# Token mixers cut into steps paced by dense tiles, block changes made token tile by token tile, and the operator set-up spread over two blocks

## The chip, the cores and the metric

One Trainium2 chip, one NeuronCore. The metric is device time of one execution in microseconds (us). The kernel before was run three times: 2354.3, 2359.55 and 2361.64 us, median 2359.55 us. One more execution was profiled and took 2362.64 us, 3.1 us more than that median; every duration read from the trace belongs to it.

## The reference, cut to what matters

One pre-norm layer over 2048 tokens of width 1024, in float32: a token mixer with four head groups of width 256, then a squared-ReLU MLP of width 4096.

```python
h = rmsnorm(x, norm_mix)
proj = h @ w_in                                  # 1024 x 2560
y_a = short_conv_mixer(cv_h, cv_b, cv_c, conv_w)         # A: gated convolution over 3 tokens
y_b = s5_mixer(s5_u, ...)                                # B: complex diagonal state space, scan, GELU, GLU
y_c = swa_sink_attention(a_q, a_k, a_v, ...)             # C: attention over 3 chunks of 64 tokens, with sinks
y_d = hgrn2_mixer(hg_q, hg_f, hg_i, hg_g, ...)           # D: gated linear recurrence, 4 heads of 64
y = rmsnorm(stack([y_a, y_b, y_c, y_d]), group_norm)
x = x + y @ w_out
h = rmsnorm(x, norm_ffn)
x = x + square(relu(h @ w_ff1)) @ w_ff2
```

B and D carry a state along the tokens, C reads the two chunks before its own, A the two tokens before.

## The kernel before, in words

**Dense work.** Every dense product is made of matmuls of 128x128 by 128x512. Each float32 operand is split into a high and a low part of a reduced type, and `mm3` (L485) adds three products: high by high (L486), high by low (L487), low by high (L488). A *dense tile* is one bank of 512 accumulated columns: 8 blocks of the contraction, so 24 matmuls. The 2048 tokens go in four blocks of 512. Per block and in `w_in`: `attn_in` (L668) 4 tiles, `hgrn_in` (L800) 4, `hgrn_in2` (L821) 4, `conv_group` (L516) 6, `s5_in` (L570) 2, so 20 tiles; then `outp` (L941) 8 tiles per block with `w_out`. That makes 112 tiles in the *mixer stage*. `attn_in`, `hgrn_in2` and `outp` go by token tile (`tm_tile`, L505: the 128 tokens are stationary, one tile reads one quarter of the activations); `hgrn_in`, `conv_group` and `s5_in` go by feature tile (`proj_fm`, L494: each reads all 512 tokens).

**Weights.** `load_split` (L98) loads a unit of 128x512, ACT writes the high part (L105), DVE the low part (L111). A tile needs two new units on average (224 units in all). Rings hold 6 raw units and 9 split ones. Matmul tiles have two PSUM banks (`mm`), transposes of activations one (`tr`), attention two (`mx`), the recurrence two (`hx`), the state space one (`sx`).

**Activations.** `hh` and `hl` (L140) hold one block's normalised, transposed, split activations, and there is one copy of them. `make_hT` (L464) fills them with 8 transposes per token tile through `tr`; `outp` fills the same two buffers with the mixers' outputs, 6 transposes per token tile through `hx` (L959, L963, L964), from rows that the mixers have stored to HBM.

**Mixers.** `attn` (L683) per token tile: norms, transposes, then per key head scores, softmax, transposes of the probabilities, product with the values. `hgrn` (L837) per half block: seven levels of doubling length, each of masked products (L877 to h=8, L880 above), their evacuation (DVE L886 or ACT L889), and three multiplies that prepare the next level (DVE L895, POOL L896, DVE L898), then state products. `s5_setup` (L211) computes the operators of the state space once, nearly all of it many short DVE instructions; `s5_step` (L580) takes two blocks at a time: eight channel groups, then eight gated-unit tiles, whose results go to HBM. `conv_finish` (L547) norms the convolution. `rstd_of` (L89) does every reciprocal root, on POOL.

**Order.** All of this is traced by Python generators, which `run` (L979) exhausts one after the other (L989 to L1041); a `yield` has no effect there. The order of tracing is the order of priority. A scheduler then gives each engine one fixed order: among the instructions whose inputs it reckons to be ready, the one with the highest priority goes first, and dense matmuls fill in where a mixer is reckoned to wait. `tc.high_priority()` lifts the weight splits and the evacuations; `first(HTP)` lifts `make_hT` above the rest of its block. Per block the list is: activations, dense tiles of attention and recurrence, `hgrn`, `attn`, then the convolution's and the state space's dense tiles, `s5_step` after blocks 1 and 3. `s5_setup` lies in block 0, `outp` after all blocks. SP issues every load and store from one queue.

After L1041 come the two MLP stages (`ff1` with L1189, the second product at L1319). The change does not touch them.

Of the kernel before, what the change touches and what calls it, by code (L numbers as in the profile page):

```python
# [21 lines left out]
P = 128  # L22
# [37 lines left out]
def emit(ctx, tc, a):  # L60
# [150 lines left out]
    def s5_setup():  # L211
        with tc.tile_pool(name="st", bufs=1) as st:
# [106 lines left out]
            dbl(cs, sn)  # L319

# [15 lines left out]
            for k in range(2, 9):  # L336
                h1, h2 = k // 2, k - k // 2
                cmul(pw[:, 0, :, k], pw[:, 1, :, k], pw[:, 0, :, h1], pw[:, 1, :, h1], pw[:, 0, :, h2], pw[:, 1, :, h2])
            rv = st.tile([P, 2, 8, 8], F32, name="rv")
            for k in range(8):  # L340
                V.tensor_copy(out=rv[:, :, :, k], in_=pw[:, :, :, 7 - k])

# [24 lines left out]
            tt(bb[:, 1], bb[:, 1], tb_, ALU.add)  # L367

# [11 lines left out]
            while n < P:  # L380
# [10 lines left out]
                n *= 2  # L391
            V.tensor_copy(out=rotN[:, 0, :], in_=ctab[:, :, P])
# [7 lines left out]
            def outer(xr, xi, pr, pi, neg):  # L400
# [3 lines left out]
                for q in range(2):  # L404
# [11 lines left out]
                    if neg:  # L416
                        stt(f3(o1), f3(o1), -1.0, f3(tmp), ALU.mult, ALU.subtract)
                    else:
                        tt(o1, o1, tmp, ALU.add)
                return o  # L420
# [3 lines left out]
            E = outer(cc[:, 0], cc[:, 1], pw[:, 0, :, 0:8], pw[:, 1, :, 0:8], True)  # L424
            tt(db, db, ident[0:16, 0:16].unsqueeze(1).to_broadcast([16, 16, 16]), ALU.mult)
            for q4 in range(4):
                H = st.tile([16, 4, 16, 8], F32, tag="H", name="H")
                for par in range(2):
                    ph = psum_sx()
                    rs = slice(par * 64, par * 64 + 64)  # L430
                    for gl in range(2):
                        gp = q4 * 2 + gl
                        for i_ in range(2):
# [3 lines left out]
                                  in_=ph[0:16, 0:256].rearrange("p (g n) -> p g n", g=2))  # L437
                tt(H[:, :, :, 0], H[:, :, :, 0], db[:, q4 * 4:(q4 + 1) * 4, :], ALU.add)
                for i_ in range(8):
                    Hs = st.tile([16, 4, 16, 8], F32, tag="Hs", name="Hs")  # L440
                    if i_ > 0:
# [3 lines left out]
                                 in_=Hs.rearrange("p (q g) h k -> p q (g h k)", g=2))  # L445

            E = outer(cc[:, 0], cc[:, 1], pw[:, 0, :, 1:9], pw[:, 1, :, 1:9], True)
# [6 lines left out]
            E = outer(bb[:, 0], bb[:, 1], rv[:, 0], rv[:, 1], False)  # L454
            for gp in range(8):
# [5 lines left out]
                SY.dma_start(out=two_d[:, gp, 2:4, :], in_=wsb)  # L461


    def make_hT(b):  # L464
        for i in range(4):
# [6 lines left out]
            V.scalar_tensor_tensor(out=xt, in0=xt, scalar=r, in1=g_mix, op0=ALU.mult, op1=ALU.mult)  # L472
            for k4 in range(2):
# [73 lines left out]
    def conv_finish(b):  # L547
# [4 lines left out]
        V.tensor_tensor(out=sq[0], in0=sq[0], in1=sq[1], op=ALU.add)  # L552
        pss = psum_tr()
        for i in range(4):
# [6 lines left out]
                        in1=r.unsqueeze(2).to_broadcast([P, 4, P]), op=ALU.mult)  # L561
        pb = psum_tr()
# [17 lines left out]
    def s5_step(s):  # L580
        newc = cm.tile([P, 8, 2], F32, tag="carry2", name="carry2")
        for gp in range(8):
# [27 lines left out]
            yield  # L610
# [9 lines left out]
            if s == 0:  # L620
# [4 lines left out]
                V.tensor_tensor(out=newc[:, gp, 1:2], in0=k1[:, 1:2], in1=k1[:, 2:3], op=ALU.add)  # L625
            py = psum_sx()
# [17 lines left out]
        for j in range(NCH):  # L644
            yt = s5p.tile([P, 2, P], F32, tag="yt", name="yt", bufs=2)
            SY.dma_start(out=yt, in_=g_d[s][:, j, :].rearrange("(c p) n -> p c n", p=P))
            yh = s5p.tile([P, 2, P], F32R, tag="yh", name="yh")
            yl = s5p.tile([P, 2, P], F32R, tag="yl", name="yl")
            S.activation(out=yh, in_=yt, func=AF.Copy)
            V.tensor_tensor(out=yl, in0=yt, in1=yh, op=ALU.subtract)  # L650
            pg = psum_sx()
            for ct in range(2):
                mm3(pg, yh[:, ct, :], yl[:, ct, :], wgh[:, ct, :], wgl[:, ct, :], ct == 0, ct == 1)
            th = s5p.tile([P, GW], F32, tag="ta", name="gth")
# [6 lines left out]
            yo = s5p.tile([P, GW], F32, tag="gyo", name="gyo")  # L661
# [21 lines left out]
    def attn(b):  # L683
# [4 lines left out]
        for i in range(4):  # L688
# [7 lines left out]
            sq = mix.tile([P, 384], F32, tag="qsq", name="qsq")  # L696
# [12 lines left out]
                            in1=r[:, 4:6].unsqueeze(2).to_broadcast([P, 2, 64]), op=ALU.mult)  # L709
            pt = psum_mx()  # L710
# [10 lines left out]
            for kv in range(2):  # L721
# [23 lines left out]
                pT = psum_mx()  # L745
# [617 lines left out]
```

## Time and profile before

| | |
|---|---|
| median of three runs | 2359.55 us |
| profiled execution, its own time | 2362.64 us |
| its span, first to last instruction | 2360.9 us |
| mixer stage, to the first MLP matmul | 0 to 1042 us |
| first MLP product | 1042 to 1728 us |
| second MLP product | 1728 to 2361 us |
| PE, DVE, ACT, POOL busy share of the span | 95%, 61%, 41%, 7% |

The span is the time that the trace covers; the 1.7 us between it and the execution's own time lie around it. "Busy" of PE counts a matmul from its start to its modelled end, and neighbours overlap, so a busy PE may still be one that waits for its pipeline. PEclk is the granted clock of TensorE as a share of 2.4 GHz; its other level is 1.2 GHz, so 0.75 over a stretch means that half of the stretch ran at the lower level.

### The profile page before, as it was taken

The numbers are of one execution on the slowest core, as the hardware profiler recorded it, in microseconds if no ns is written. First come the engines' busy times: TensorE is split into PE (matmuls) and PEld (weight loads), VectorE is DVE, ScalarE is ACT, GpSimd is POOL, SyncE is SP. The second block draws the span as 40 slices with busy tenths as digits, with TensorE's granted clock in tenths as the row PEclk, the third lists the DMA queues.
The fourth block names the chain that finished last, engine by engine and source line by source line (L and its number), as shares of the span: only waits on it lengthen the run. The fifth ranks groups of instructions, "written<-read, shape, count | busy, mean of one in ns | idle before, by whom it ended". The sixth has DMA issues, their size and how long they took to land.

```text
span 2360.9 us, 32548 instructions
## 1 busy us (share of the span) xinstructions
PE 2240.9 (95%) x11460; PEld 1751.5 (74%) x11460; DVE 1447.0 (61%) x3008; ACT 956.5 (41%) x1910; POOL 166.5 (7%) x208
## 2 busy tenths in 40 slices
PE   7899998999999998999999999999989999999999
PEld 6676776666777776777777767777768888888887
DVE  6688687887656775586656666766653344244342
ACT  4334333434434334465555564544543133133121
POOL 1130112023113000000000000000000000000000
PEclk9999997999999999999999999999999999999999
DMA  6313324441331566656566577888774554455542
GB/s 203 85 49 113 111 78 124 140 121 56 106 103 47 154 217 199 216 174 190 176 180 177 179 213 252 284 258 259 215 222 144 172 183 137 131 187 177 185 147 98
DMA packets 393347, 381.35 MB, mean 162 GB/s; under 512 B 35968, under 2 KB 310496, under 8 KB 393184
## 3 DMA queue, kind: packets, MB, share of 16 engines
q1 hardware_dynamic: 393184, 379.27, 51.8%
q8 instruction: 90, 1.47, 0.3%
q14 instruction: 73, 0.60, 0.1%
HBM read 261.77 MB, written 116.40 MB: 160 GB/s over the span
## 4 chain that ended last, share of the span: by engine, by line
PE 60%; DVE 10%; DMA 7%; ACT 4%; issue 3%; POOL 2%; SPq 0%; DVEq 0%; POOLq 0%; ACTq 0%
PE mm L1319 25%; PE mm L1189 10%; PE hx L1189 5%; PE mm L488 4%; PE mm L487 4%; PE mm L486 4%; DMA w2r<-in_w_ff_dram 2%; PE mx L1189 2%; DVE tp L1060 2%; ACT wh L1050 1%; DVE w2r L1060 1%; DMA fxs<-x1d 1%; DMA wr<-in_w_out_dram 1%; DVE wl L1051 1%; PE mx L778 1%
## 5 line engine op out<-in xcount | busy, mean ns | idle before, releaser
L1319 PE MATMUL mm<-wh,st 128*128 128x512 f32 x1792 | 561.9, 394 | 0.9 <-ACT X L1322 0.7
L1319 PEld LDWEIGHTS mm<-wh,st 128*128 128x128 f32 x1792 | 337.3, 188 | 79.8 <-ACT X L1322 1.2
L1319 PE MATMUL mm<-wl,st 128*128 128x512 f32 x896 | 353.5, 395 | 2.7 <-DVE wl L1051 2.7
L1189 PE MATMUL mm<-tb,wh 128*128 128x512 f32 x1024 | 330.0, 403 | 16.4 <-ACT tp L1202 6.7
L1290 ACT ACTIVATE st<-sr 128x1024 fp32r<-128x1024 f32 x112 | 114.6, 1054 | 404.2 <-PE mm L1319 359.2
L1189 PEld LDWEIGHTS mm<-tb,wh 128*128 128x128 f32 x1024 | 189.5, 191 | 77.2 <-ACT tp L1208 14.2
L487 PE MATMUL mm<-wl,hh 128*128 128x512 f32 x512 | 205.2, 401 | 4.8 <-DVE wl L111 4.8
L486 PE MATMUL mm<-wh,hh 128*128 128x512 f32 x512 | 206.9, 404 | 2.2 <-ACT hh L481 2.1
L1051 DVE TENSOR_TENSOR wl<-wr,wh 128x512 fp32r<-128x512 f32 x208 | 138.0, 687 | 113.6 <-ACT wh L1050 66.7
L488 PE MATMUL mm<-wh,hl 128*128 128x512 f32 x512 | 207.3, 405 | 0.0
L105 ACT ACTIVATE wh<-wr 128x512 fp32r<-128x512 f32 x224 | 138.6, 629 | 168.2 <-PE mm L487 111.7
L1189 PE MATMUL mm<-tb,wl 128*128 128x512 f32 x512 | 204.2, 399 | 0.0
L1319 PEld LDWEIGHTS mm<-wl,st 128*128 128x128 f32 x896 | 168.4, 188 | 43.1 <-DVE wl L1051 3.1
L1291 DVE TENSOR_TENSOR st<-sr,st 128x1024 fp32r<-128x1024 f32 x112 | 133.8, 1221 | 95.0 <-ACT st L1290 94.9
L111 DVE TENSOR_TENSOR wl<-wr,wh 128x512 fp32r<-128x512 f32 x224 | 152.4, 698 | 40.1 <-ACT wh L105 36.9
L1189 PE MATMUL hx<-tb,wh 128*128 128x512 f32 x512 | 162.4, 397 | 8.4 <-ACT wh L1050 8.4
L486 PE MATMUL mm<-hh,wh 128*128 128x512 f32 x384 | 157.1, 409 | 2.0 <-ACT QP L807 1.0
L488 PE MATMUL mm<-hh,wl 128*128 128x512 f32 x384 | 157.1, 409 | 0.0
L487 PE MATMUL mm<-hl,wh 128*128 128x512 f32 x384 | 156.3, 407 | 0.0
L1050 ACT ACTIVATE wh<-wr 128x512 fp32r<-128x512 f32 x208 | 125.7, 625 | 69.3 <-PE mm L1189 31.2
L1060 DVE TENSOR_TENSOR tq<-mm,tq 128x512 f32<-128x512 f32 x32 | 22.1, 691 | 173.6 <-PE mm L1319 173.4
L1195 ACT ACTIVATE tp<-tp 128x512 f32<-128x512 f32 x96 | 60.5, 630 | 157.1 <-DVE tp L1060 157.1
(372 smaller groups left out, 3638.3 us busy)
## 6 DMA issues: line engine op xcount, KB each, us to landing
as<-tp SPq DMA_DIRECT2D x224, 256.0 KB, 2.8
sr<-as SPq DMA_DIRECT2D x112, 512.0 KB, 4.3
wr<-in_w_ff_dram SPq DMA_DIRECT2D x176, 256.0 KB, 3.9
wr<-in_w_in_dram SPq DMA_DIRECT2D x160, 256.0 KB, 3.1
wr<-in_w_out_dram SPq DMA_DIRECT2D x64, 256.0 KB, 4.0
w2r<-in_w_ff_dram SPq DMA_DIRECT2D x32, 512.0 KB, 4.5
tt<-w2r SPq DMA_DIRECT2D x32, 512.0 KB, 3.3
wr<-tt SPq DMA_DIRECT2D x64, 256.0 KB, 4.2
```

Source lines behind the costliest of these rows:

```text
L105: S.activation(out=hi, in_=raw, func=AF.Copy)
L111: (G if le == "p" else V).tensor_tensor(out=lo, in0=raw, in1=hi, op=ALU.subtract)
L486: PE.matmul(ps, lhsT=lh, rhs=rh, start=first, stop=False)
L487: PE.matmul(ps, lhsT=lh, rhs=rl, start=False, stop=False)
L488: PE.matmul(ps, lhsT=ll, rhs=rh, start=False, stop=last)
L1050: S.activation(out=h, in_=raw, func=AF.Copy)
L1051: V.tensor_tensor(out=l, in0=raw, in1=h, op=ALU.subtract)
L1060: V.tensor_tensor(out=o, in0=x, in1=y, op=op)
L1189: PE.matmul(ps, lhsT=(wh, wl)[lw][:, ks], rhs=b[lb][:, k, :], start=first and k == 0 and q == 0, stop=k == 3 and q == 2, skip_group_check= ...
L1290: S.activation(out=s_[:, 0, ks], in_=r, func=AF.Copy)
L1291: V.tensor_tensor(out=s_[:, 1, ks], in0=r, in1=s_[:, 0, ks], op=ALU.subtract)
L1319: PE.matmul(ps, lhsT=st_[:, ls, k, :], rhs=tu[i, k][lt], start=k == 0 and p_ == 0, stop=k == NJ - 1 and p_ == 2)
```

## The change

The generators get more `yield`s, so that one step of a mixer is some PE work whose inputs were made in the step before, followed by the vector work for the next. A small driver replaces the list of `run` calls: after every dense tile, each mixer on a list of *tracks* advances by its own pace.

```diff
+    def track(gen, pace, key):
+        tracks.append([gen, pace, 0.0, key])
+    def advance():
+        for t_ in list(tracks):
+            t_[2] += t_[1]
+            while t_[2] >= 1.0:
+                t_[2] -= 1.0
+                if next(t_[0], "end") == "end":
...
+    def dense(g, side=None):
+        for _ in g:
+            if side is not None:
+                next(side, None)
+            advance()
...
+    for b in range(NB):
+        dense(attn_in(b))
+        drain("hg")
+        track(attn(b), 1.35, "at")
+        if b == 0:
+            track(s5_setup(), 1.5, "set")
+        if b == 2:
+            drain("set")
+            s5p = mixs.enter_context(tc.tile_pool(name="s5p", bufs=1, reuse_waits="tile"))
+            track(s5_step(0), 1.0, "s5")
+        if b == 3:
+            drain("s5")
+            dense(s5_in(b))
+            track(s5_step(1), 1.0, "s5")
+        dense(hgrn_in(b))
+        track(hgrn(b), 1.25, "hg")
+        dense(conv_group(b))
+        track(conv_finish(b), 0.5, "cv")
+        if b < 3:
+            dense(s5_in(b))
+        nxt = make_hT(b + 1) if b < 3 else out_in(0)
+        next(nxt)
+        dense(hgrn_in2(b), nxt)
+        run(nxt)
+        drain("at", "cv")
+    for b in range(3):
+        g = outp(b)
+        for _ in range(4):
+            next(g)
+            advance()
+        drain(*((), ("s5",), ("hg",))[b])
+        nxt = out_in(b + 1)
+        next(nxt)
+        dense(g, nxt)
+        run(nxt)
```

`drain` runs what is left of a track at once. The side generator makes the block change: after token tile i of `hgrn_in2` (or of the second half of `outp`) the next block's token tile i is transposed into the quarter of `hh` and `hl` that has just been read. Its load and norm are traced one tile ahead.

```diff
     def make_hT(b):
+        def norm(i):
...
+        nx = norm(0)
+        yield
+        for i in range(4):
+            xt = nx
+            if i < 3:
+                nx = norm(i + 1)
...
-    def outp(b):
+    def out_in(b):
...
+        nx = load(0)
+        yield
+        for i in range(4):
...
-                    pt = psum_hx()
+                pt = psum_tr()
```

In `hgrn` the two halves of a block now alternate level by level instead of following one another; a level is one step, and the state part waits until `hgrn_in2` has been traced.

```diff
-        for hf in range(2):
-            yield from hgrn_half(b, hf, QPs[hf], KQs[hf], Fgs[hf], ...)
...
+        for lv in range(7):
+            for hf in range(2):
...
+                bps[hf] = nbp
+                yield
+        while ("hv", b) not in st8:
+            yield
...
-            ke = mix.tile([P, GW], F32, tag="ke", name="ke", bufs=2)
+            ke = mix.tile([P, 2, GW], F32, tag="ke", name="ke")
```

`hacc` gets four buffers for two, the small products `bp` two for one. In `attn`, the load shift and the norm of token tile i+1 are traced in the last step of tile i before its probabilities are transposed, and there is a `yield` before the transposes of the probabilities and one after their evacuation. In `s5_step`, the gated unit's load and split (`glu_in`) are traced one tile ahead with two buffers, and the step boundary of a channel group lies after all its scan work. In `s5_setup` there are yields between its parts (some 45 steps). The priority lift of `outp`'s transposes goes; its evacuations keep theirs. The same products are computed; no arithmetic is added.

## Rows read from the trace of the kernel before

**Rows 1.** The page's head: span, busy time of engines, granted clock in 40 slices.
```profile
span 2360.9 us, 32548 instructions
...
PE 2240.9 (95%) x11460; PEld 1751.5 (74%) x11460; DVE 1447.0 (61%) x3008; ACT 956.5 (41%) x1910; POOL 166.5 (7%) x208
...
PEclk9999997999999999999999999999999999999999
```
**Rows 2.** Windows by stage: length, busy PE, PEld, DVE, ACT, POOL, clock, DMA.
```profile
0.00:13.00 13.00, 1.11 (x4) 0.71 (x4) 3.68 (x15) 5.42 (x9) 1.31 (x6) 1.00 0.71 246
13.00:200.00 187.00, 169.43 (x1105) 131.18 (x1105) 137.81 (x472) 71.81 (x190) 36.97 (x41) 0.95 0.36 99
200.00:390.00 190.00, 178.65 (x1156) 136.69 (x1154) 144.31 (x354) 69.06 (x176) 33.08 (x38) 0.92 0.36 102
390.00:610.00 220.00, 205.77 (x1408) 153.13 (x1407) 175.17 (x515) 93.40 (x266) 44.41 (x56) 0.99 0.38 110
610.00:785.00 175.00, 165.09 (x1161) 128.41 (x1160) 107.24 (x268) 70.95 (x194) 36.16 (x41) 1.00 0.29 87
785.00:1042.00 257.00, 241.23 (x1192) 186.28 (x1191) 174.66 (x385) 106.19 (x229) 10.18 (x18) 0.99 0.64 205
1042.00:1728.00 686.00, 654.80 (x2759) 509.92 (x2758) 448.93 (x698) 363.94 (x628) 4.39 (x8) 0.99 0.70 213
1728.00:2361.00 633.00, 624.82 (x2688) 505.17 (x2686) 255.24 (x307) 175.70 (x225) 0.00 (x0) 1.00 0.49 161
```
**Rows 3.** Windows inside the mixer stage: length, busy PE, PEld, DVE, ACT, POOL, clock, DMA.
```profile
100.00:175.00 75.00, 66.38 (x647) 50.77 (x644) 68.83 (x291) 28.87 (x94) 23.20 (x28) 1.00 0.15 45
350.00:400.00 50.00, 43.95 (x332) 33.73 (x332) 37.80 (x93) 15.36 (x44) 8.11 (x10) 0.73 0.41 113
...
525.00:600.00 75.00, 67.70 (x619) 50.70 (x618) 56.77 (x162) 33.53 (x111) 23.16 (x30) 1.00 0.21 59
...
650.00:675.00 25.00, 25.00 (x112) 20.71 (x111) 11.25 (x25) 8.73 (x20) 0.00 (x0) 1.00 0.46 139
...
925.00:940.00 15.00, 8.85 (x35) 6.69 (x34) 5.78 (x10) 3.81 (x8) 0.00 (x0) 0.78 0.83 286
```
**Rows 4.** Groups of instructions by line, whole run: busy us, mean ns, idle before.
```profile
L488 PE MATMUL mm<-wh,hl 128*128 128x512 f32 x512 | 207.3, 405 | 0.0
...
L488 PE MATMUL mm<-hh,wl 128*128 128x512 f32 x384 | 157.1, 409 | 0.0
...
L111 DVE TENSOR_TENSOR wl<-wr,wh 128x512 fp32r<-128x512 f32 x224 | 152.4, 698 | 40.1 <-ACT wh L105 36.9 <-ACT apr L741 1.5 <-PE mm L488 0.2
...
L886 DVE COPY_PREDICATED hacc<-masks,hx 128x512 f32<-128x512 uint8 x64 | 43.9, 725 | 8.8 <-PE hx L877 8.6
...
L964 DVE TENSOR_TENSOR hl<-hx,hh 128x384 fp32r<-128x384 f32 x32 | 17.2, 552 | 17.2 <-ACT hh L963 16.8
...
L963 ACT ACTIVATE hh<-hx 128x384 fp32r<-128x384 f32 x32 | 15.1, 487 | 31.8 <-PE mm L487 19.3 <-PE hx L959 11.5 <-PE mm L488 0.6
```
**Rows 5.** PE's waits from 13 to 785 us: total us, times, longest us.
```profile
PE hx L877 <- DVE QP L895: 7.3, 6, 2.3
PE mm L487 <- DVE wl L111: 4.8, 2, 2.6
...
PE tr L477 <- DVE hl L482: 2.6, 6, 0.8
```
**Rows 6.** Timeline of PE, 925 to 938 us: start, us, instruction, idle before it.
```profile
935.59 1.54 PE L959 MATMUL hx<-ident,ybt 128*128 128x128 f32 x6 [6.07 <-DMA ybt<-ybd]
```
**Rows 7.** Line L896, POOL's multiply of the recurrence: ns least, median, most.
```profile
L896 POOL TENSOR_TENSOR KQ<-KQ,bp x48: 614/688/955, 105.0 to 757.4; 128x256 f32<-128x256 f32 x48
```
**Rows 8.** SP's queue in the mixer stage: its longest wait in total.
```profile
SPq L102 <- DVE wl L111: 164.2, 115, 17.2
```

More of the change, by code (lines that the diff above doesn't have):

```diff
@@ L367, in s5_setup @@
             tt(bb[:, 1], bb[:, 1], tb_, ALU.add)
+            yield
             for _ in range(3):
@@ L687, in attn, with norm @@
             V.tensor_copy(out=kT[:, 0:P], in_=st8["ktail"])
-        for i in range(4):
+        def norm(i):
             ti = b * 4 + i
@@ L695, in attn @@
                 SY.dma_start(out=st8["vs"][64:128, :], in_=va[0:64, :])
-            sq = mix.tile([P, 384], F32, tag="qsq", name="qsq")
+            prev = (st8.get("va"), st8.get("vs"))
+            st8["va"], st8["vs"] = va, vs_next
+            sq = mix.tile([P, 384], F32, tag="qn", name="qsq")
             S.activation(out=sq, in_=qk, func=AF.Square)
@@ L744, in attn @@
                 V.reciprocal(out=rs_, in_=rs_)
-                pT = psum_mx()
-                pTs = mix.tile([P, 2, 2, P], F32, tag="pTs", name="pTs")
                 vvs = []
@@ L756, in attn @@
                     elif e == 0:
-                        parts = [(0, 128, st8["va"]), (128, 64, va)]
+                        parts = [(0, 128, va_prev), (128, 64, va)]
                     else:
-                        parts = [(0, 128, st8["vs"]), (128, 64, vs_next)]
+                        parts = [(0, 128, vs_prev), (128, 64, vs_next)]
                     vvs.append(parts)
-                    for pi, (o, kn, vv) in enumerate(parts):
+                if kv == 1 and i < 3:
+                    nx = norm(i + 1)
+                yield
+                pT = psum_mx()
+                pTs = mix.tile([P, 2, 2, P], F32, tag="pTs", name="pTs")
+                for e in range(2):
+                    for pi, (o, kn, vv) in enumerate(vvs[e]):
                         o2 = (pi * 2 + e) * P
@@ L983, in run @@
         return r
-    def hT(b):
-        with first(-4000 if b == 0 else HTP):
-            run(make_hT(b))
-    hT(0)
-    run(hgrn_in2(0))
-    run(hgrn_in(0))
-    run(attn_in(0))
-    run(hgrn(0))
-    run(attn(0))
-    s5_setup()
-    s5p = mixs.enter_context(tc.tile_pool(name="s5p", bufs=1, reuse_waits="tile"))
-    run(conv_group(0))
-    run(conv_finish(0))
-    run(s5_in(0))
-    hT(1)
-    run(attn_in(1))
-    run(hgrn_in(1))
-    run(hgrn_in2(1))
-    run(hgrn(1))
-    run(attn(1))
@@ L1006, in emit @@
-    run(conv_group(1))
-    run(conv_finish(1))
-    run(s5_in(1))
-    run(s5_step(0))
-    hT(2)
-    run(attn_in(2))
-    run(hgrn_in(2))
-    run(hgrn_in2(2))
-    run(hgrn(2))
-    run(attn(2))
-    run(conv_group(2))
-    run(conv_finish(2))
-    run(s5_in(2))
-    hT(3)
-    run(attn_in(3))
-    run(hgrn_in(3))
-    run(hgrn_in2(3))
-    run(hgrn(3))
-    run(attn(3))
-    run(conv_group(3))
-    run(conv_finish(3))
-    run(s5_in(3))
-    run(s5_step(1))
-    run(outp(0))
-    run(outp(1))
@@ L1031, in emit, with drain @@
-    run(outp(2))
+    tracks = []
+    def track(gen, pace, key):
[6 more added lines that the diff above has]
+                if next(t_[0], "end") == "end":
+                    tracks.remove(t_)
+                    break
+    def drain(*keys):
+        for t_ in list(tracks):
+            if t_[3] in keys:
+                run(t_[0])
+                tracks.remove(t_)
@@ new lines, in dense @@
+    def dense(g, side=None):
[3 more added lines that the diff above has]
+            advance()
+    with first(-4000):
+        run(make_hT(0))
+    s5p = None
+    for b in range(NB):
[23 more added lines that the diff above has]
+        drain("at", "cv")
```

274 lines of the change are left out of this document (152 added, 122 removed).

## The prediction

> **What bounds the kernel now.** I read the page's head first. PE is busy for 95% of the span, DVE for 61%, POOL for 7% [rows 1]. So only PE's idle time, its lower clock, and waits hidden inside its busy time can be won; no product is taken away.
>
> The windows by stage come next [rows 2]. The two MLP stages, 686 and 633 us, are not touched; there PE idles 686 - 654.8 = 31.2 us (4.5%) and 633 - 624.8 = 8.2 us (1.3%). In the mixer stage PE starts dense work at 13 us, and from there to 1042 us, 1029 us long, it is busy 169.4 + 178.7 + 205.8 + 165.1 + 241.2 = 960.2 us. It idles **68.8 us**, 6.7%. The stage's clock is also the only one with real dips: 0.95 over 187 us and 0.92 over 190 us lose 9.4 and 15.2 us of full-speed time, 0.01 of the 220 and 257 us another 4.8: **29.3 us** in all.
>
> Then where these lie [rows 3]. From 100 to 175 us DVE is busy 68.8 of 75 us (92%) and PE idles 8.6 us: block 0's recurrence, attention and the operator set-up are crowded there. From 650 to 675 us DVE works 45% and PE runs 112 matmuls in 25 us without a gap, 0.223 us each. The dense stage is 112 tiles of 24, 2688 matmuls: lines L488 count 512 + 384, and two sister lines as many each [rows 4], so 600 us at that rate, 5.36 us per tile. The other 360 busy us are small matmuls. What is wrong is the distribution: mixers come in lumps, with few dense tiles beside them, and pure dense stretches lie between.
>
> PE's waits name the chains [rows 5]: QP's multiply before a level's products, the split before a transpose's bank is free. Each is small. The largest single one is 6.07 us at 929 us, where the last output block's rows come back from HBM [rows 6].
>
> **The change, part by part.** All numbers are against the profiled execution's 2362.6 us, which lies 3.1 us above the median of 2359.55 that I predict from.
>
> *Pacing.* Dense tiles per block 20, 5.36 us each. `attn` has 22 steps at 1.35 per tile (16 tiles), `hgrn` 15 steps on 12 tiles at 1.25 and the rest on the next block's 4, `s5_setup` some 45 steps on 30 tiles, `s5_step` 25 on 20 to 26. So each step's inputs are about one tile older than its matmuls, against a DVE chain of two L886 (1.45 us) and a multiply, plus POOL's 0.69 us [rows 4, 7]. That covers the waits before small matmuls [rows 5], if DVE has no backlog. DVE's work stays at 739 us over the stage; on 970 us that is 76%, without the 92% lump. How much idle time stays, no row shows. The ends are the MLP stages' shares on 973 us: 44 us at 4.5%, where DVE is busy 65%, and 13 us at 1.3%, where it is busy 40% [rows 2]. With 76% it is nearer the first; I take (2 x 44 + 13)/3 = 34 us left, **35 us back**. Below: nothing back.
>
> *Clock.* The deepest dip, 0.73 from 350 to 400 us, came with PE busy 44 of 50 us but nearly all of that on small matmuls (332 matmuls where pure dense work shows 112 per 25 us); from 525 to 600 us dense tiles and small groups mix, and the clock is 1.00 [rows 3]. Paced steps are such a mix everywhere. Ends 0 and 29.3; nearest is the mixed row, so all but 5 us come back, **24 us**. The Trainium skill ("TensorE: Matmul & The Clock Gate", section "Why this matters for your kernels") puts drops down to idle gaps between bursts of matmuls. That agrees with the 6.07 us gap followed by 0.78 [rows 3, 6], not with the dip of a busy PE; by it only 0.22 x 15 = 3.3 us would come back and the sum would be 21 us worse.
>
> *Block change by token tile.* Before, the transposes of the next block wait for the last feature tile, which reads all 512 tokens; now each hides behind the next token tile's 24 matmuls. Its idle time is part of the 68.8. `out_in` moves from the two `hx` banks to the single `tr` bank: 16 token tiles, each with a second group that waits for ACT 0.49 + DVE 0.55 = 1.04 us [rows 4]: 0 to 16.6 us. `make_hT` lives with the same one bank and shows 2.6 us over its 16 tiles [rows 5]; I take **+3**. Queued behind such a transpose on PE are dense tile i+1 and the steps traced with it. Loads for the next tile join SP's queue one tile earlier; there they pass weight loads that mostly wait for a free raw buffer (164 us over 115 waits [rows 8]) and are early by 5.36 us, so nothing is added. The 6.07 us should mostly go: it needs the last gated unit's store, which the drain inside `outp(1)` puts just ahead of the load, so up to 1 or 2 us can remain; counted in the 34.
>
> *Drains.* A handful of steps are left at each: one of `hgrn`, one of `attn`, five gated-unit tiles in block 3. They run as chains, with dense tiles of `s5_in(3)` as cover; without it a 0.7 us DVE link each. **+1**.
>
> *Set-up spread, `norm` and `glu_in` a tile early.* The DVE count is the same; the short set-up instructions leave the stretch of 92%. Early norms put POOL's root ahead of recurrence multiplies on POOL, which is busy 162 of the 1029 us [rows 2]; cover is ample. The set-up's many small stores pass the weight loads in SP's queue over 30 tiles instead of 20; both are waited for a tile later. Merging two copies of `ke` into one, and alternating halves, save ACT time that nobody waits for. All nothing; if the cover goes, it is the price of the slower rival.
>
> *Inside busy time.* A small matmul whose predecessor feeds it is counted busy while its pipe fills. No row gives that share of the 360 us. Between 0 and one twentieth (18 us) could come back with fewer, longer groups; I take none and keep 18 for the range.
>
> **Sum:** -35 - 24 + 3 + 1 = -55 us: 2307.6 against 2362.6, so about **2304 us** against the median.
>
> **Rivals.**
>
> *Clock dips stay.* If small matmul groups pull the clock down wherever they are, only 3.3 of the 24 us return: 2304 + 21 = 2325. For it: 0.73 with PE busy. Against it: 1.00 in the mixed row. This is also where the skill's rule on idle gaps leads. Chance 0.12.
>
> *The order hardly changes.* The scheduler already mixes dense and mixer matmuls by readiness; tracing in other order may give the same interleaving, and DVE, not the order, makes the chains late. Then little beyond the 6 us gap returns: 2353. For it: 95% busy already. Against it: DVE at 92% and 45% in stretches of the same stage [rows 3]. Chance 0.12, half of it within 0.3% (7 us, about what a measurement can tell from no change).
>
> *Slower: mixer work on DVE in front of the weight split.* Now every dense tile has mixer instructions around it, in one DVE order with the split L111 (0.70 us, two per tile, nine buffers, of which a token tile group holds eight). If one L886 (0.725 us) is exposed per tile, 112 x 0.725 = 81 us come in against 55: 2386 us. It decides at 55/112 = 0.49 us per tile. Behind the late split stand the tile's 24 matmuls, its evacuation, and the raw buffer that SP's next weight load waits for. For it: 68.8 of 75 us where everything meets. Against it: until 785 us PE waits only 4.8 us in total for L111 [rows 5]. Chance 0.12. The Trainium skill ("SBUF — State Buffer", section "SBUF: two separate sides") has a further way to it: a GpSimd instruction and a DVE one with two SBUF inputs lock each other out of a shared port. L896 between 614 and 955 ns [rows 7] fits some of that, with POOL as the loser; no row shows DVE losing.
>
> *Larger gain.* Idle falls to 13 us (56 back), all 29 us of clock, no added cost: -85, 2275; with the 18 us inside busy time 2257. For it: 25 us without a gap at 650 us. Against it: nothing runs that smoothly with DVE above 70%. Chance 0.08.
>
> **How the numbers follow.** The forecast has 0.56 and lies between 2280 and 2335. Faster by over 0.3%: 0.56 + 0.12 + 0.06 + 0.08 = 0.82; same 0.06; slower 0.12. The range takes in the larger gain's end and the rivals up to no change: 2257 to 2360; left out are the slower rival and a little at either end.
>
> **What would show it.** The first L1189 matmul should come near 987 us instead of 1042, the MLP stages staying at 686 and 633. In windows of the mixer stage DVE should lie between 60 and 90% everywhere, PE's idle sum from 13 us near 34, the clock at 0.98 or more in each stage; waits of `hx` and `mx` matmuls for DVE should shrink and those of `tr` grow a little (L959's successor). It is wrong if PE's wait for L111 exceeds 50 us, if the clock stays at 0.95 or below in the first 400 us, or if an MLP stage moves by more than 5 us.

## The result, and the profile after

The change makes the kernel **faster by half a per cent**: median 2346.52 us of 16 executions (2338.22 to 2357.89) against 2359.86 us of 16 executions of the kernel before; ratio **0.9949**, 95% interval [0.9932, 0.9965]. That is 12 us by the ratio (13 between the medians) where 55 were forecast. The profiled execution has a span of 2341.6 us, 19.3 less than that of [rows 1]; its own time, 2343.7 us, lies 2.8 us under the median, and that of the profiled execution before 2.8 us above the median of its kernel, so the shares below add up to 19 and not to 12.

The page's head, to be read beside [rows 1]:

```profile
span 2341.6 us, 32446 instructions
...
PE 2227.5 (95%) x11460; PEld 1761.9 (75%) x11460; DVE 1433.2 (61%) x3008; ACT 949.8 (41%) x1902; POOL 163.2 (7%) x208
...
PEclk9899999999999999999999999999999999999999
```

The windows of the kernel after answer to [rows 2] (length, busy PE, PEld, DVE, ACT, POOL, clock, DMA). The mixer stage now ends at 1019 us, the first MLP product at 1711:

```profile
13.00:200.00 187.00, 167.48 (x1079) 130.75 (x1079) 139.00 (x476) 72.30 (x192) 28.84 (x33) 0.94 0.37 104
200.00:400.00 200.00, 192.40 (x1313) 147.58 (x1312) 149.74 (x388) 80.21 (x216) 40.69 (x48) 1.00 0.40 112
400.00:600.00 200.00, 191.84 (x1356) 152.38 (x1355) 153.98 (x449) 80.16 (x219) 37.08 (x44) 1.00 0.39 109
600.00:800.00 200.00, 189.85 (x1282) 148.42 (x1280) 148.36 (x414) 77.98 (x224) 33.83 (x43) 0.97 0.39 113
800.00:1019.00 219.00, 206.03 (x997) 166.82 (x994) 128.89 (x259) 90.01 (x187) 17.06 (x26) 0.98 0.60 196
1019.00:1039.00 20.00, 15.33 (x60) 11.39 (x59) 19.92 (x34) 13.46 (x26) 0.00 (x0) 0.90 0.45 136
1019.00:1711.00 692.00, 653.22 (x2754) 508.92 (x2753) 453.12 (x703) 367.04 (x632) 4.39 (x8) 0.99 0.69 212
1711.00:2341.00 630.00, 625.20 (x2691) 505.86 (x2689) 255.80 (x308) 176.04 (x227) 0.00 (x0) 1.00 0.49 162
```

Between 200 and 800 us DVE is now busy 74 to 77% in every row, where the rows before lay between 61 and 80%. The lump that the prediction named, from 100 to 175 us, is nearly as high as it was (68.83 of 75 us before):

```profile
100.00:175.00 75.00, 69.10 (x559) 53.79 (x559) 66.45 (x205) 24.30 (x70) 16.20 (x18) 0.98 0.25 72
```

PE is busy 947.6 of the 1006 us from 13 to 1019, so it idles 58.4 us where the kernel before idled 68.8: 10 us back, not 35. The clock loses 0.06 x 187 + 0.03 x 200 + 0.02 x 219 = 21.6 us instead of 29.3: 8 back, not 24. The rows show where: from 200 to 400 us the loss of 15 us is gone; up to 200 us it is 11 where it was 9; behind 600 us, where the kernel before lost 3, it is 10. PE's busy time of the stage falls by 960.2 - 947.6 = 12.6 us, of which the clock can be 8; the prediction took none for this term and kept up to 18 for the range. The first MLP product is 6 us longer (idle 38.8 us, before 31.2), the second 3 us shorter.

PE's waits from 13 to 1019 us (total us, times, longest) answer to [rows 5]:

```profile
PE mx L810 <- DVE apr L790: 11.2, 10, 2.9
PE mx L770 <- DVE kT L760: 9.1, 2, 8.6
PE tr L1016 <- DVE hl L1021: 5.8, 6, 2.0
...
PE hx L921 <- DVE hacc L930: 3.4, 2, 2.3
PE tr L500 <- DVE hl L505: 3.0, 6, 0.9
```

The recurrence's waits (L877 then, L921 now) and the 6.07 us of [rows 6] are nearly gone; no wait of PE for the weight split L111 is left at all. In their place stand attention's transposes of the probabilities (L810, which wait for the softmax's last scaling), one wait of 8.57 us at the keys (L770), and the output rows' transposes in the single `tr` bank (L1016). A single execution's clock varies, so the table takes the mean of each kernel's compared executions (of the kernel before, those that ran beside the first twelve experiments); "clock" is (1 - granted clock) x span, "rest" the span without it.

| kernel | executions | granted clock | span | clock, us | rest, us |
|---|---|---|---|---|---|
| before | 45 | 0.9839 | 2359.0 | 38.0 | 2320.9 |
| after | 16 | 0.9855 | 2345.8 | 34.0 | 2311.8 |
| one go | 4 | 0.9815 | 2391.8 | 44.3 | 2347.6 |
| blocks whole | 12 | 0.9812 | 2364.3 | 44.3 | 2320.0 |
| early `ldt` | 6 | 0.9875 | 2338.3 | 29.2 | 2309.0 |
| two `hx` banks | 6 | 0.9882 | 2333.0 | 27.6 | 2305.4 |
| both of these | 6 | 0.9875 | 2328.4 | 29.1 | 2299.3 |
| every third split on POOL | 5 | 0.9742 | 2385.9 | 61.6 | 2324.3 |

So of the change's gain **4 us are clock and 9 us the rest**. Among the 16 executions of the kernel after, spans run from 2336.2 us (clock 0.989) to 2355.8 us (0.982).

### The profile page after: what moved, and what is told of

Read it like the earlier page. It is cut to its first block, busy times and chain, and to the rows that moved or that the text cites. A ratio compares the mean times of both kernels' runs of the same rounds, so it can differ in the third digit from the quotient of the medians.

```text
span 2341.6 us, 32446 instructions
## 1 busy us (share of the span) xinstructions
PE 2227.5 (95%) x11460; PEld 1761.9 (75%) x11460; DVE 1433.2 (61%) x3008; ACT 949.8 (41%) x1902; POOL 163.2 (7%) x208
## 4 chain that ended last, share of the span: by engine, by line
PE 67%; DVE 13%; DMA 9%; ACT 4%; issue 3%; POOL 2%; SPq 1%; DVEq 0%; POOLq 0%; ACTq 0%
PE mm L1397 26%; PE mm L1267 10%; PE mm L509 5%; PE mm L511 5%; PE mm L510 5%; PE hx L1267 5%; DMA w2r<-in_w_ff_dram 2%; DVE wl L111 2%; PE mx L1267 2%; DVE tp L1138 2%; PE hx L921 1%; DMA fxs<-x1d 1%; PE mx L826 1%; ACT wh L1128 1%; DVE w2r L1138 1%
## 5 line engine op out<-in xcount | busy, mean ns | idle before, releaser
L111 DVE TENSOR_TENSOR wl<-wr,wh 128x512 fp32r<-128x512 f32 x224 | 151.3, 694 | 30.5 <-ACT wh L105 26.3
```

The source lines that it names most:

```text
L111: (G if le == "p" else V).tensor_tensor(out=lo, in0=raw, in1=hi, op=ALU.subtract)
```

## The experiments

The theory after the first look: pacing does what it says, but three costs were sized too small (the single `tr` bank, a load that DVE now stands for, the chain of attention), and the clock follows something other than the share of small matmuls. The rivals: the order hardly matters; DVE is the bound.

**One go.** Each mixer is traced whole where its track starts.

```diff
     def track(gen, pace, key):
-        tracks.append([gen, pace, 0.0, key])
+        if key == "hg":
+            for _ in range(15):
+                next(gen)
+            tracks.append([gen, 0.0, 0.0, key])
+        else:
+            run(gen)
```

> The changed kernel with its driver changed alone: each mixer is traced in one go where its track starts (the recurrence's 15 level steps there, its state part at the old drain), so the set-up lies wholly in block 0 again. Theory A (pacing brings the gain, by moving small matmul groups away from the dense matmul that must wait for them): the mixer stage, which ends at 1019 us in the changed kernel and at 1042 in the one before, ends between 1035 and 1050, the ratio to before is between 0.998 and 1.005, and DVE is above 90% busy from 100 to 175 us again. Theory B (the scheduler interleaves by readiness whatever the tracing order, and the gain of 0.5% came from the block change): the stage ends within 5 us of 1019, ratio 0.993 to 0.997.

Measured: 2394.09 us, 1.0147 [1.0126, 1.0168], 47 us slower than the kernel after and slower than either theory had it (the stage ends at 1074 us, by theory A at 1035 to 1050). So within the new driver the tracing order matters much. But one go is not the kernel before: it is 35 us slower than that too, so the 47 us are not what the change won. The stage's one window, in this kernel:

```profile
13.00:1074.00 1061.00, 997.72 (x6016) 768.70 (x6017) 722.61 (x1985) 406.64 (x1038) 155.18 (x194) 0.96 0.41 122
```

And paced:

```profile
13.00:1019.00 1006.00, 947.60 (x6015) 745.96 (x6015) 719.98 (x1984) 400.66 (x1036) 157.50 (x194) 0.98 0.43 129
```

The stage is 55 us longer: idle time adds only 63.3 - 58.4 = 5 us and the clock some 20, by rows rounded to 0.01; the other 30 lie inside busy time. PE's groups of the stage show the largest part, the recurrence's levels, first in one go (busy us, mean ns, idle before):

```profile
L921 PE MATMUL hx<-QP,KQ 64*128 64x128 f32 x512 | 74.2, 306 | 1.7 <-DVE hacc L930 1.1
```

The same group of the kernel after:

```profile
L921 PE MATMUL hx<-QP,KQ 64*128 64x128 f32 x512 | 56.4, 293 | 6.1 <-DVE hacc L930 3.4 <-DVE ctab L217 2.5
```

And the same products in the kernel before:

```profile
L877 PE MATMUL hx<-QP,KQ 64*128 64x128 f32 x512 | 42.1, 300 | 13.0 <-DVE QP L895 7.3 <-DVE anm L735 2.8 <-DVE ars L743 1.1
```

So in the kernel after this group waits less than before, 6.1 us against 13.0, but is busy 14 us longer. Neighbours overlap, so these 14 us need not be lost time; whether alternating the halves brings them was not tried.

**Blocks whole.** The block change is taken back alone: `dense(hgrn_in2(b), nxt)` becomes `dense(hgrn_in2(b))`, `dense(g, nxt)` becomes `dense(g)`, so that the next block's transposes follow the last token tile.

> The changed kernel with the block change undone alone: the next block's transposes are traced after the last token tile of hgrn_in2 (and of the output product), not beside its token tiles. Theory A: the block change is worth 5 to 10 us of the 12 us, ratio to before 0.998 to 0.999, with idle time of PE at the four block changes in blocks and the four in the output part. Theory B: it is worth all of it or more, ratio 1.000 to 1.005. If the scheduler reorders it anyway: 0.995, within 2 us.

Measured: 2366.22 us, 1.0025 [1.0010, 1.0041], 0.0076 above the kernel after, some 18 us: 10 of clock and 8 of the rest by the table. That is theory B's range and not A's: without this part the change loses 6 us against the kernel before, and its rest, 2320.0 us, is what it was there (2320.9). The 18 us are the worth of the block change in this kernel, where the transposes that it uncovers go through the single `tr` bank. What the other parts win no more than covers what they cost; two of these costs are measured next.

**Early `ldt`.** The two small loads of `s5_log_dt` (2 KB each) go from the head of `s5_setup` to the constants.

```diff
+    ldt = cm.tile([P, 8], F32, name="ldt")
+    for g2 in range(2):
+        SY.dma_start(out=ldt[g2 * 64:(g2 + 1) * 64, :],
...
-            ldt = small("ldt")
-            for g2 in range(2):
-                SY.dma_start(out=ldt[g2 * 64:(g2 + 1) * 64, :],
...
```

> The changed kernel with one load moved: the state space's log_dt (two scattered loads of 4-byte pieces) is issued with the constants at the start instead of in the set-up's first step. Theory A (DVE stands 11.4 us for this load in front of kT, PE then idles 8.6 us and runs at the lower clock for part of 50 to 100 us): the gap goes, the clock from 50 to 100 us rises from 0.80 to 0.95 or more, the mixer stage ends 10 to 16 us earlier, ratio to before 0.988 to 0.991. Rival C (DVE is the bound, a stall only shifts its backlog): under 3 us, ratio 0.994 to 0.995.

Measured: 2339.69 us, 0.9924 [0.9906, 0.9942], 6 to 7 us below the kernel after and between the two theories (the clock from 50 to 100 us rises from 0.80 to 0.88, the stage ends 8 us earlier). The two intervals overlap, but the same step on top of the next experiment gives 4 to 7 us again (below). What it removes is plain in the timelines of the kernel after, DVE's first (start, us, instruction, idle before it):

```profile
61.73 0.17 DVE L223 TENSOR_SCALAR t<-ldt 128x8 f32<-128x8 f32 x1 [11.41 <-DMA ldt<-in_s_log_dt_dram]
...
68.18 0.35 DVE L760 TENSOR_SCALAR kT<-mx,kgain 128x128 f32<-128x128 f32 x1
```

And PE's:

```profile
68.59 1.22 PE L770 MATMUL mx<-kT,qT 64*128 64x64 f32 x4 [8.57 <-DVE kT L760]
```

DVE stands 11.41 us for the load, which takes 11.0 us from issue to landing. Behind it on DVE's one queue stands the evacuation of attention's keys, after 6.4 us of other DVE work that had queued up (61.73 to 68.18), and for that PE waits 8.57 us. With the early load PE's waits for `kT` are 2.9 us in all, DVE's for `ldt` none. The wait for the softmax shrinks too, to about half:

```profile
PE mx L810 <- DVE apr L790: 5.7, 9, 1.1
```

The Trainium skill ("DMA: Bandwidth & Descriptors", section "Rules for kernel authors") says that a strided or non-contiguous last dimension becomes one descriptor per element, and that a DMA should be issued early and waited for late. The early load agrees with the second; no run here shows what makes these 2 KB take 11 us.

**The same in the kernel before.**

> The kernel before with log_dt loaded with the constants, nothing else. There the same 11.7 us stand of DVE falls into the dense tiles of attention in block 0, where PE waits 4.8 us for weight splits and the clock is 0.90. Theory A (the stand costs the kernel before less, because no mixer step is due behind it): 2 to 6 us, ratio 0.997 to 0.999. If it costs as much as in the changed kernel: 0.994 to 0.996. If it is covered: 1.000.

Measured: 2361.49 us, 1.0004 [0.9991, 1.0017]. There DVE stood as long, 11.7 us, with weight splits behind it, and PE did wait for these: the 4.8 us for L111 of [rows 5] end at 71.4 and 74.5 us, right behind the stand. The early load removes them, and in its profile another wait takes their place (waits of ACT and of PE from 13 to 200 us):

```profile
ACT wh L105 <- DMA wr<-in_w_in_dram: 10.7, 1, 10.7
...
PE mm L486 <- ACT QP L807: 5.2, 1, 5.2
```

Now ACT stands 10.7 us for a weight load, and PE waits 5.2 us for an evacuation further back in ACT's order. So the load's wait held up PE there too, and taking it away gained nothing. Whether the early load itself made the weight load late was not tried.

**Two `hx` banks.** `out_in` takes its old banks back; the rest of the change stays.

```diff
-                pt = psum_tr()
+                pt = psum_hx()
```

> The changed kernel with the transposes of out_in on the recurrence's two PSUM banks again, as in the kernel before, instead of the single tr bank. My prediction's term for the single bank was 3 us; PE's waits for the split that frees it are 5.8 us in the trace of the changed kernel, and its weight loads' 10 us. Theory A: 3 to 8 us come back, ratio to before 0.9915 to 0.9940. Rival C: below 2 us, since dense tiles go in front of the waiting transposes.

Measured: 2333.58 us, 0.9899 [0.9878, 0.9919], 0.0050 below the kernel after, **12 us**, more than the 3 to 8 expected. The 5.8 us of L1016's wait for `hl` leave PE's list. By the table half of the gain is rest (6.4 us), half clock (6.4 us).

**Both.** Early `ldt` and two `hx` banks.

> The changed kernel with both earlier edits: log_dt loaded with the constants, and out_in's transposes on the recurrence's two banks. Theory A (the two costs lie in different places, block 0 and the output part, and add): mixer stage ends at 1019 - 8 - 12 = 999 us, ratio to before 0.992 + 0.990 - 0.995 = 0.987, 2330 us. Rival (both are given back at the start of the first MLP product, where DVE is the bound): ratio 0.990.

Measured: 2329.97 us, **0.9868** [0.9848, 0.9888], the best of all and where the two savings add, some 30 us below the kernel before and 17 below the kernel after. Its stage, first and second product:

```profile
13.00:1008.00 995.00, 949.85 (x6015) 748.93 (x6016) 721.58 (x1987) 399.50 (x1037) 160.48 (x194) 0.97 0.44 130
...
1008.00:1695.00 687.00, 651.07 (x2752) 507.14 (x2752) 451.28 (x701) 366.40 (x631) 4.39 (x8) 0.99 0.69 213
1695.00:2325.00 630.00, 624.12 (x2691) 504.72 (x2689) 255.82 (x308) 176.10 (x227) 0.00 (x0) 1.00 0.50 162
```

Idle in the stage is now 995 - 949.85 = 45 us, 11 above the forecast's 34.

**Is attention's chain what is left?** Six kernels, three on the kernel after and three on the best one. In *half tiles* the tracks advance twice per dense tile, by half the pace:

```diff
+            if k == 4:
+                advance()
...
-            t_[2] += t_[1]
+            t_[2] += t_[1] / 2
```

> The changed kernel with the same paces applied at half tiles: the tracks advance by half their pace after 12 of a tile's 24 matmuls and after 24. At tile ends alone, a pace of 1.35 traces two steps of attention together after every third tile, 1.25 two of the recurrence after every fourth. Theory D (steps traced together are what PE waits for: the second's inputs are fresh): PE's wait before the probabilities' transposes, 12.8 us over 11 times in the changed kernel, falls below 6, ratio to before 0.988 to 0.992. Rival E (the softmax chain between two attention steps, two reductions, three exponentials and two scalings over DVE and ACT, is longer than the 4 us that 1.35 leaves per step however the steps are spread): that wait stays at 9 us or more, ratio 0.993 to 0.997.

Measured: 2340.91 us, 0.9915 [0.9891, 0.9940]. The wait (L815 here) is 5.1 us, and both numbers are theory D's; but the interval overlaps that of the kernel after, and by the means over executions 4 of the 6 us are clock. *Half tiles and a gap* has one more empty `yield` between the softmax and the transposes of its probabilities, at a pace of 1.85 for 1.35:

> As the half-tile kernel, with one more empty step between each softmax and the transposes of its probabilities, and attention's pace raised from 1.35 to 1.85 so that it still ends with its block. The softmax chain then has two steps (5.8 us) and the short links 2.9 us. Theory E (the chain is longer than a step): the wait before the probabilities' transposes falls below 4 us in total, ratio to before at most 0.990. Theory D (double steps alone): no better than the half-tile kernel. Rival C (DVE's backlog decides): the waits move to other small groups, ratio 0.993 to 0.997.

Measured: 2339.96 us, 0.9924 [0.9896, 0.9951]. L810's wait falls from 11.2 to 2.9 us, and the wait for the keys grows from 9.1 to 12.1. Theory E's wait went, its time did not come. *Norm in two* cuts attention's norm behind its root, so that DVE need not stand for POOL:

> The changed kernel with attention's early norm cut in two: squares, sums and POOL's root in the last softmax step, the two scalings that need the root one step later. In the changed kernel DVE stands 18.6 us in 15 times for that root, 3.9 us in the kernel before. Theory F (DVE's stand for POOL is what makes later steps late): DVE's wait for qrs falls below 6 us and 3 to 8 us come back, ratio to before 0.9915 to 0.9940. Rival: DVE has slack there, within 2 us, 0.994 to 0.996.

Measured: 2345.52 us, 0.9932 [0.9909, 0.9955], and nothing decided: the edit did not do what it was made for, DVE still waits 17.3 us for that root, 18.6 without the cut. On the best kernel, *half tiles*:

> log_dt early, out_in on two banks, and half-tile paces together. If the three savings add (8 us of half tiles, 6 and 12 us of the others, each against the changed kernel's 0.995): ratio to before 0.983 to 0.985, about 2323 us. If half tiles only repaired waits that the early log_dt repairs as well (attention's waits in block 0): 0.986 to 0.988, as without them.

and *half tiles and a gap*:

> As the last, with the empty step after each softmax and attention at 1.85. Theory E: the softmax chain longer than a step still costs in the blocks 1 to 3, so 2 to 5 us better than the last one, ratio 0.981 to 0.984. Otherwise the same as the last within 2 us, or worse where the closer other steps wait.

Measured: 2333.97 us, 0.9893 [0.9870, 0.9916], and 2339.04 us, 0.9923 [0.9894, 0.9951]: no better than the best kernel (0.9868), the second worse. Neither of the two ranges expected of the first holds. Last, the gap with whole tiles, on the best kernel:

> The version with the early load and the two hx banks, and one empty step between the softmax and the transposes of its probabilities, attention's pace raised from 1.35 to 1.85 for it; whole-tile pacing as in the change. If attention's chain holds what is left of the idle time, TensorE's wait at the transposes of the probabilities falls from 4.7 us to under 2 and the ratio from 0.987 to 0.985 or less. If waits only change places, as in the half-tile versions, that wait falls, another one takes its place, and the ratio stays at 0.986 to 0.991.

Measured: 2338.22 us, 0.9910 [0.9890, 0.9930], slower than the best kernel by some 8 us. L810's wait hardly moved (4.7 us to 4.0), and another came first; PE's waits of this kernel:

```profile
PE hx L922 <- DVE hacc L931: 8.3, 4, 2.7
PE mx L811 <- DVE apr L790: 4.0, 7, 1.1
```

So no version turned attention's wait into time: where it shrank most, the keys' wait grew, and on the best kernel, where the early load had already halved it, more room hardly changed it.

**Is DVE the bound?** On the best kernel, every third weight split goes to POOL: `LO = "d"` becomes `LO = "ddp"`.

> log_dt early and two banks (0.987 alone), and every third weight unit's low part made on POOL instead of DVE, some 75 of 224 units, about 50 us of DVE's 740 in the mixer stage. Theory C (DVE's queue is what still makes PE's small groups late): idle time of PE falls by 10 us or more, ratio 0.980 to 0.984. Rival G (latencies of chains, not DVE's load): no gain, and POOL's slower subtraction makes tiles wait for weights, ratio 0.987 to 1.000.

Measured: 2387.87 us, 1.0120 [1.0100, 1.0140], 58 us slower than the best kernel. The line's own view (ns least, median, most) shows the price:

```profile
L111 DVE TENSOR_TENSOR wl<-wr,wh x150: 662/684/1807, 11.3 to 1037.0; 128x512 fp32r<-128x512 f32 x150
...
L111 POOL TENSOR_TENSOR wl<-wr,wh x74: 1261/1297/4119, 12.4 to 1033.1; 128x512 fp32r<-128x512 f32 x74
```

POOL takes 1.9 times as long, and more for some. DVE did 74 splits less, and PE waited longer: for the softmax (L810) 17.4 us against 4.7, for `make_hT`'s bank (L500) 6.9 against 3.2. That does not clear DVE altogether, since POOL's part of the chains grew too; but lightening DVE in this way buys nothing. The ratio lies above both ranges expected. The other half of the rival is not borne out: PE shows no wait for L111 in this kernel. By the table 32 of the 58 us are clock, 61.6 us lost against 29.1.

**What lowers the clock?** Gaps and small matmuls, put into the second MLP product of the kernel after, whose clock is 1.00. A chain of DVE instructions multiplies a result by zero, several times over, and adds it to the next tile's operand; a burst of 64x64 products, used by nothing, goes to a free bank.

```diff
+                stall(X[:, q], {1: 0, 3: 2, 5: 5}.get(q))
...
+                    for n in range(200):
+                        PE.matmul(pj[0:64, n % 8 * 64:n % 8 * 64 + 64], lhsT=X[0:64, 0, 0:64],
+                                  rhs=X[0:64, 1, 0:64], start=True, stop=True)
```

> Base: the kernel after. In the second MLP product, whose clock is 1.00 in the kernels before and after, TensorE is made to wait three times for chains of 2, 4 and 7 short VectorE instructions (about 0.7 us each, so gaps of some 2, 3.5 and 5.5 us, 11 us in all), and at one other place it runs 200 extra matmuls of 64x64 in a row with nothing to wait for (332 matmuls in 43.95 busy us are 0.132 us each, so about 26 us). Theory A, idle gaps lower the clock: the window behind the longest gap, perhaps behind the second, shows 0.7 to 0.9 and the window of the burst 1.00; the stage grows by 11 + 26 us and by 3 us or more of lost clock per gap that counts. Theory B, small matmuls lower it (the prediction's reading of the dip at 350 to 400 us): the burst and the 25 us behind it show about 0.73, 7 to 13 us lost, and the windows behind the gaps stay at 1.00. In both the run lies 35 to 55 us above the kernel after, some 1.01 of before.

Measured: 2377.84 us, 1.0059 [1.0037, 1.0081], some 26 us above the kernel after where 35 to 55 were expected. The scheduler spoiled the first half: it filled the gaps with the burst, and no gap over 0.8 us arose. The clock was 1.00 in every window of the burst's pieces, the longest of 196 small matmuls in a row. So once more, with a burst twice as long that reads a tile made later, and chains of 2, 6 and 11 instructions:

```diff
-                stall(X[:, q], {1: 0, 3: 2, 5: 5}.get(q))
+                stall(X[:, q], {1: 0, 3: 4, 5: 9}.get(q))
...
-                    for n in range(200):
+                    for n in range(400):
```

> As the kernel with gaps and a burst, where the small matmuls had filled the gaps; here they read a tile that is made only after the last of the three chains, and there are 400 of them (800 instructions of 0.060 us, so about 48 us in one or two pieces). The chains have 2, 6 and 11 VectorE instructions of 0.35 to 0.7 us, so gaps of about 1, 3 and 6 us. Idle gaps lower the clock (theory A): 1.00 in the burst, and after the longest gap, perhaps after the middle one, a stretch at 0.50 of 3 to 10 us, each costing half its length. Small matmuls lower it (theory B): a lower clock in or behind the burst and none behind the gaps. The stage grows by 48 + 10 us, and by 2 to 10 us of clock under A.

Measured: 2414.36 us, 1.0230 [1.0199, 1.0260], as theory A had it. PE's timeline, three pieces, with the gaps in brackets:

```profile
1925.16 0.47 PE L1407 MATMUL mm<-wh,st 128*128 128x512 f32 x1 [2.70 <-DVE st L1392]
...
1953.33 0.76 PE L1407 MATMUL mm<-wh,st 128*128 128x512 f32 x1 [5.55 <-DVE st L1392]
...
1985.74 0.77 PE L1407 MATMUL mm<-wh,st 128*128 128x512 f32 x1 [7.91 <-DVE st L1392]
```

and the windows around them and over the burst (length, busy PE, clock, DMA):

```profile
1922.00:1939.00 17.00, 14.30 (x62) 1.00 0.19 62
...
1950.70:1957.50 6.80, 4.17 (x10) 0.50 0.45 154
1957.50:1977.00 19.50, 19.50 (x86) 1.00 0.21 67
1981.40:1991.60 10.20, 5.86 (x14) 0.50 0.31 100
1991.60:2020.00 28.40, 28.40 (x124) 1.00 0.51 160
2056.00:2103.00 47.00, 47.00 (x802) 1.00 0.08 24
```

**Here long idle gaps do it, 64x64 matmuls without gaps don't.** After 2.70 us the clock stays at 2.4 GHz in this place. The gaps of 5.55 and 7.91 us bring 6.8 and 10.2 us at 1.2 GHz, which begin inside the gap. Of these, 4.2 and 5.9 us (1957.5 - 1953.3 and 1991.6 - 1985.7) lie behind its end, half of which is lost: 2 to 3 us on top of the gap itself. The burst, 47 us of nothing but small matmuls, keeps the full clock.

## Why the prediction was right in sign and wrong in size

**Right.** Faster, and the block change by token tile hides its transposes. The 6.07 us gap went but for a 1.2 us wait for `ybt`. The slower rival fell: PE's wait for L111 was to decide it and is nil. That the order hardly changes fell with the first experiment. The forecast lies 42 us below the median measured, which stands between two of the rivals; these steps failed:

*Pacing brings 35 + 24 us, the block change no more than a part of the 35.* Taken back alone, the block change is worth 18 us, more than the whole net gain, and the kernel without it is 6 us slower than the kernel before, at the same rest. If the two costs below add there as they do in the best kernel, pacing without them and without the block change stands at an estimated 10 to 13 us of gain, not 59. The lump of DVE that was to go stayed, 89% against 92%.

*Clock: 24 us back.* 4 us came, by the mean of the executions. The step that failed is the reading of the dip at 350 to 400 us as the work of small matmuls, from a busy share of 44 in 50 [rows 3], and the conclusion that a mix of dense tiles and small groups keeps the clock full. That dip did go, and from 200 to 600 us the paced kernel's clock is 1.00, as forecast; but dips stand ahead of 200 us (0.94) and, where there were hardly any before, behind 600 us (0.97 and 0.98). Nor was PE's busy time in that row nearly all small matmuls. The dense ones alone (tile `mm`), in the row's 50 us and inside the dip:

```profile
350.00:400.00 50.00, 15.69 (x58) 0.73 0.41 113
363.00:391.00 28.00, 0.77 (x1) 0.51 0.26 75
```

A window of 50 us hides what stands just ahead of the dip. In the kernel before, PE's timeline there:

```profile
362.94 0.33 PE L458 MATMUL sx<-ident,E 128*128 128x128 f32 x1 [1.72 <-DVE E L217]
364.93 0.69 PE L458 MATMUL sx<-ident,E 128*128 128x128 f32 x2 [1.66 <-DVE wsb L460]
```

And two windows, inside the dip and ahead of it (length, busy PE, clock, DMA):

```profile
363.00:391.00 28.00, 23.69 (x210) 0.51 0.26 75
340.00:363.00 23.00, 21.28 (x106) 1.00 0.55 145
```

Two gaps in a row stand where a clock of 1.00 ends, and 28 us at the lower level follow; PE idles 4.3 of these too. Why the level stays low for so long is not shown. The Trainium skill ("TensorE: Matmul & The Clock Gate", section "Why this matters for your kernels") puts drops down to idle gaps between bursts of matmuls. The experiment with gaps agrees (1.00 after 2.70 us, 0.50 with 5.55 us). Yet in the kernel before dips also follow single waits of 2 us, and not all of them. Two of PE's waits there:

```profile
182.11 0.79 PE L763 MATMUL mx<-ident,apr 128*128 128x128 f32 x4 [2.31 <-DVE apr L749]
...
703.02 1.16 PE L877 MATMUL hx<-QP,KQ 64*128 64x128 f32 x16 [2.26 <-DVE QP L895]
```

And what follows each (length, busy PE, clock, DMA):

```profile
182.20:193.00 10.80, 10.80 (x45) 0.53 0.12 37
703.00:715.00 12.00, 11.82 (x157) 1.00 0.07 23
```

The rival "clock dips stay" had nearly the right size, 3.3 us back, in part by luck: the dip that it kept went, and others came. Its reason, that small groups wherever they are pull the clock down, does not hold for the burst. The paced kernel removes many short waits and brings one gap of 8.57 us.

*Idle time: 35 us back.* 10 came. The forecast took the idle share of the MLP stages over to a stage whose steps are chains through DVE, ACT, POOL and PE. One tile of distance covers the recurrence's chain; the softmax's L810 still waits 11.2 us, about half of it because of the late load of the set-up (5.7 with the early load). What is left cannot simply be bought off, as the versions with half tiles and with a gap show.

*The single `tr` bank: 3 us, bounds 0 to 16.6.* It cost 12, inside the bounds. The 2.6 us of `make_hT` [rows 5] were the wrong nearest row: those transposes hide behind `hgrn_in2` with mixer steps between, while `out_in` falls into `outp`, where fewer tracks are left. That last reason is argued, not tried.

*The set-up spread: 0 us.* It cost 4 to 7, because the load that DVE stands for met the keys' evacuation. The prediction did name what to ask, what is queued behind a waiting instruction, but asked it of the set-up's stores and the early norms and not of its first load. The price that it gave for lost cover, 81 us, was far off.

*MLP stages unchanged.* The first product is 6 us longer, over the 5 allowed. In its first 20 us after 1019 DVE is busy 19.92 and PE 15.33 us, with one wait of 3.8 us in PE's list:

```profile
PE mm L1267 <- DVE tb L1198: 3.8, 1, 3.8
```

An operand's split was not done when PE got there. Before, PE was busy for all of the first 20 us. That the stage ended sooner does not explain it: in the best kernel it ends sooner still, at 1008 us, and the product takes 687 us. The cause is open.

With the two costs taken out, the best kernel stands 26 us above the forecast. Idle time is 11 us of it (45 against 34, one profile), the clock 15 (24 forecast, 38.0 - 29.1 = 9 returned, means over executions). That these add up to 26 is partly chance: the forecast still held 3 us for the single bank, and the two terms come from different executions. The drains' +1 us cannot be told apart from these.

**Open.** Which short gaps lower the clock: single ones of 2.26 and 2.70 us did not, one of 2.31 and a pair of 1.7 stand ahead of a dip; length alone does not decide. How far the rest of the idle time could fall: no version with more room for a chain got time from it on the best kernel. An earlier start of the MLP's preparation was not tried.

## What to carry to other kernels

Price idle time gap by gap and not by its sum: the gaps of 5.55 and 7.91 us cost 2 to 3 us more than themselves by the clock, and evening out many short waits returned only 4 us of clock here. Before reading a dip, look at PE's waits just ahead of it. Take parts of a change back one by one before crediting one of them: here the net gain needs both, without the block change the kernel is 6 us slower than the kernel before, without the pacing 35. When work is spread out, look at every load that an in-order engine stands for and ask what will stand behind it *after* the move, and try to issue it early: that brought 4 to 7 us here, and nothing in the kernel before, where another wait took its place. A part of the change that takes a second buffer away (two banks to one) deserves its own run: taking that one line back doubled the gain.

## What was not expected of the hardware

A load of 2 KB that takes 11.0 us to land and holds DVE for 11.4; a clock that stays full through 47 us of 64x64 matmuls with no 512-column product among them; and executions of one kernel whose clock differs between 0.982 and 0.990 and whose span goes with it, over 19 us, more than the whole gain of the change.
